# A two-block model kernel: loads in order of use, S5 by blocks, borders k by k, the tail by halves

## The chip, the cores and the metric

The kernel runs on one core of a Trainium2 chip. The metric is the device time of one execution in microseconds (us); the median of three runs is compared. A core has five engines with queues of their own that run in order: TensorE (PE in the profile) for matmuls, VectorE (DVE), ScalarE (ACT), GpSimd (POOL) and SyncE (SP), which here only issues DMAs. ACT and POOL issue DMAs too; in the profile ACTq and SPq are those issues. PSUM, where matmuls accumulate, is used as eight banks of 512 fp32 columns.

## What is computed

One sequence of 512 tokens, width 1024, goes through two different blocks, all in fp32:

```python
def first_block(x, c, ...):
    mod = (silu(c) @ w_ada + b_ada).reshape(Bsz, 6, D)      # shift, scale, gate, twice
    h = modulate(rmsnorm(x, norm_mix), shift_m, scale_m)
    proj = h @ w_in
    y_pool = pool_mixer(proj[..., :s_z], ...)
    y_ssd = ssd_mixer(proj[..., s_z:s_xbc], proj[..., s_xbc:s_dt], proj[..., s_dt:], ...)
    x = x + gate_m * (concatenate([y_pool, y_ssd]) @ w_out)
    h = modulate(rmsnorm(x, norm_ffn), shift_f, scale_f)
    x = x + gate_f * peer(h, w_query, sub_keys1, sub_keys2, expert_down, expert_up)
    return rmsnorm(x, norm_final)

def second_block(x, meta_tokens, ...):
    h = concatenate([meta, x])                              # 16 + 512 tokens
    proj = rmsnorm(h, g_mix_pre) @ w_in                     # q, k, v, r, a_low, u, z_gla, z_ssm
    o = gla_chunked(q, k, v, log_sigmoid(a_low @ w_gate_up + b_gate) / 16)
    y_gla = (rmsnorm(o, gla_norm_g) * silu(r)) @ w_o_gla
    y_s = s5_ssm(u, ...)                                    # x_t = Lbar x_{t-1} + Bbar u_t ; y = Re(C x) + D u
    glu = gelu(y_s) @ w_glu + b_glu
    y_ssm = glu[..., :D] * sigmoid(glu[..., D:])
    mixed = sigmoid(z_gla) * y_gla + sigmoid(z_ssm) * y_ssm
    h = h + rmsnorm(mixed @ w_out, g_mix_post)
    f = square(relu(rmsnorm(h, g_ffn_pre) @ w_ff1)) @ w_ff2
    return (h + rmsnorm(f, g_ffn_post))[:, N_META:]
```

PEER picks for each token 8 x 16 of 16384 experts by product keys; the S5 layer has 64 groups of 16 channels with 64 complex states each.

## The kernel before

Activations stand with channels on the 128 partitions and tokens along the columns, eight tiles of 128 channels, numbered k as input and m as output. An fp32 product is made of three matmuls in fp32r (`mm3`, lines 123 to 125): operands are split into hi and lo parts, and hi x hi, hi x lo and lo x hi are summed. A weight tile of 128 x 1024 is loaded by `load_w` on SP's queue into `raw` (three buffers) and split: hi on ACT (line 115), lo on DVE (line 116). One output tile of a projection (`linear`) takes 24 matmuls of 512 columns.

The stages, in order. The start: `ada` and `ada_pe` compute the modulation from 48 weight tiles (dot products on DVE, or on PE at line 220), the input is normalised, modulated and split k by k, and three projections have their weights loaded among the modulation's. Block 1: the input projection, pooling and SSD mixers, the output projection. PEER: the modulated h is transposed for 96 tokens through ACT copies (line 544) and PE transposes (545), query projections `wq`, top-16 searches, a dense pass over all experts' down weights (128 steps j), a dense pass over the up weights (128 j; `acc`, eight banks, is summed over j), and for the first 96 tokens gathered rows on POOL. At the end of the second pass gathered sums are folded into `acc` (line 1046) and added to the residual (1048). The dense pass's operand wg is split too (line 129).

Block 2: the meta tokens are normed (line 139's sums of squares of 16 columns), the residual is scaled and split into A (Ah, Al; line 1074), squares are summed on DVE (1081) and POOL, added over partitions with ones-matmuls (1085), and the factor `sc` that the projections' results are multiplied with follows. `proj(m, put)` makes a projection over 528 tokens in two pieces of 272 and 256 columns. Four heads of gated linear attention (GLA) come first; line 1151 is the gate's matmul.

S5 (lines 1263 to 1437). The eight projections of u are multiplied with `sc` and written to DRAM (`u_d`, POOL's queue); u is read back as `u4`, 16 channels of a group by 4 time offsets on the partitions, 32 pairs of groups (line 1320, eight reads on ACT's queue). Then for each of 16 steps of two pairs: `carry` loads `mat` (ACT's queue), transposes two tables (1343), makes the kernel kk (1350, 1351), spreads it with `selt` (1356) into the block table `tbd` (DVE, 1360 and 1364, the latter adds the skip), multiplies u into the carries (1370, 1371) and scans them on DVE; `answer` multiplies tables, states and u (1405 to 1407) and copies the result over u (1408). After each second step eight writes on SP's queue bring a block of y to DRAM (1424), and `glu_in` reads it back (1306), applies gelu (1308) and splits it. Between steps PE is kept busy with `lins`: gate projections (`gate_proj`, whose z goes through DRAM, lines 1281 and 1282) and attention output projections (`gla_out`).

Then the GLU (`wglu`), `wout2`, a norm, two halves of the FFN (`wff1`, `wff2`), a norm (products at line 1510, adds at 1511) and the output's write.

The order of the work is set by a scheduler (Tile): it takes instructions by priority in a simulated time. `soon()` and `high_priority` raise priorities, tile pools with a number of buffers set what waits for what. The row numbers of the instruction order, below, count an engine's instructions.

## Time and profile before

| | us |
|---|---|
| median of three runs | 2764.64 (2762.73 to 2776.26) |
| the profiled execution | 2769.02 |
| its span, first to last instruction | 2767.2 |
| PE busy | 2649.6 |
| DVE busy | 1899.2 |
| ACT busy | 1077.0 |
| POOL busy | 450.0 |

The span is that of one profiled execution; 1.8 us lie around it. The mean granted clock of PE is 0.98 of full speed. Idle time of an engine that is not the bottleneck costs nothing, so what matters is when PE does not work, and what it waits for then.

### The profile page before, as it was taken

The numbers are of one execution on the slowest core, as the hardware profiler recorded it, in microseconds if no ns is written. First come the engines' busy times: TensorE is split into PE (matmuls) and PEld (weight loads), VectorE is DVE, ScalarE is ACT, GpSimd is POOL, SyncE is SP. The second block draws the span as 40 slices with busy tenths as digits, with TensorE's granted clock in tenths as the row PEclk, the third lists the DMA queues.
The fourth block names the chain that finished last, engine by engine and source line by source line (L and its number), as shares of the span: only waits on it lengthen the run. The fifth ranks groups of instructions, "written<-read, shape, count | busy, mean of one in ns | idle before, by whom it ended". The sixth has DMA issues, their size and how long they took to land.

```text
span 2767.2 us, 36353 instructions
## 1 busy us (share of the span) xinstructions
PE 2649.6 (96%) x13812; PEld 2359.0 (85%) x13812; DVE 1899.2 (69%) x3456; ACT 1077.0 (39%) x1541; POOL 450.0 (16%) x361
## 2 busy tenths in 40 slices
PE   6999999999999999999999899899989989999997
PEld 5877789999999999999898899777878878688885
DVE  6767699998998873898698575744546754552543
ACT  5474434444445443333432232534422243432221
POOL 0010000443333030233314120100000100110100
PEclk9999999999999999999999999999999999999999
DMA  7224324888897577989977986111365644233231
GB/s 260 85 92 152 128 85 137 296 300 324 284 337 284 204 258 249 304 303 345 319 263 259 303 298 204 62 61 62 110 150 174 202 135 136 74 94 99 91 98 62
DMA packets 176064, 531.65 MB, mean 192 GB/s; under 512 B 18320, under 2 KB 55152, under 8 KB 173968
## 3 DMA queue, kind: packets, MB, share of 16 engines
q1 hardware_dynamic: 81152, 272.15, 29.5%
q0 software_dynamic: 36912, 152.39, 15.9%
q10 hardware_dynamic: 57824, 104.78, 11.5%
q8 instruction: 108, 1.77, 0.3%
q14 instruction: 68, 0.56, 0.1%
HBM read 448.74 MB, written 80.41 MB: 191 GB/s over the span
## 4 chain that ended last, share of the span: by engine, by line
PE 81%; DMA 6%; DVE 4%; issue 4%; ACT 3%; POOL 1%; ACTq 1%; SPq 0%; DVEq 0%; POOLq 0%
PE ps L123 24%; PE ps L124 24%; PE ps L125 24%; PE ps L701 4%; DMA gt<-g_d 2%; DMA row<-in_eu_dram,gid 2%; DVE lo L116 1%; PE ps L1240 1%; DMA mats_d<-bd 1%; ACT hi L115 1%; PE ps L1243 1%; PE ps L571 1%; DVE wg L1032 0%; PE ps L1356 0%; PE ps L139 0%
## 5 line engine op out<-in xcount | busy, mean ns | idle before, releaser
L115 ACT ACTIVATE hi<-raw 128x1024 fp32r<-128x1024 f32 (+1 forms) x458 | 481.8, 1053 | 1071.1 <-PE ps L124 772.9
L116 DVE TENSOR_TENSOR lo<-raw,hi 128x1024 fp32r<-128x1024 f32 (+1 forms) x458 | 582.9, 1273 | 332.2 <-ACT hi L115 327.7
L123 PE MATMUL ps<-h2h,hi 128*128 128x416 f32 (+1 forms) x1152 | 414.2, 360 | 0.7 <-ACT hi L115 0.7
L124 PE MATMUL ps<-h2l,hi 128*128 128x416 f32 (+1 forms) x1152 | 412.6, 358 | 0.0
L125 PE MATMUL ps<-h2h,lo 128*128 128x416 f32 (+1 forms) x1152 | 411.3, 358 | 0.0
L124 PE MATMUL ps<-wl,hi 128*128 128x416 f32 x1024 | 366.5, 358 | 24.0 <-DVE wl L129 24.0
L125 PE MATMUL ps<-wh,lo 128*128 128x416 f32 x1024 | 361.2, 357 | 1.8 <-DVE lo L116 1.8
L123 PE MATMUL ps<-wh,hi 128*128 128x416 f32 x1024 | 351.8, 355 | 5.7 <-ACT wh L128 4.6
L123 PE MATMUL ps<-Ah,hi 128*128 128x512 f32 (+2 forms) x944 | 342.5, 367 | 3.1 <-ACT Ah L128 3.1
L124 PE MATMUL ps<-Al,hi 128*128 128x512 f32 (+2 forms) x944 | 341.0, 361 | 0.0
L125 PE MATMUL ps<-Ah,lo 128*128 128x512 f32 (+2 forms) x944 | 340.1, 361 | 0.5 <-DVE lo L116 0.5
L712 POOL DMA_INDIRECT row<-in_eu_dram,gid x96 | 160.5, 1672 | 420.9 <-DVE tsum L735 360.9
L123 PEld LDWEIGHTS ps<-h2h,hi 128*128 128x128 f32 x1152 | 218.0, 189 | 7.5 <-ACT hi L115 1.2
L125 PEld LDWEIGHTS ps<-h2h,lo 128*128 128x128 f32 x1152 | 217.5, 189 | 6.8 <-DVE lo L116 0.3
L124 PEld LDWEIGHTS ps<-h2l,hi 128*128 128x128 f32 x1152 | 217.8, 189 | 6.1
L124 PEld LDWEIGHTS ps<-wl,hi 128*128 128x128 f32 x1024 | 195.8, 191 | 31.6 <-DVE wl L129 27.9
L123 PEld LDWEIGHTS ps<-Ah,hi 128*128 128x128 f32 x944 | 180.1, 191 | 38.6 <-issue 7.7
L125 PEld LDWEIGHTS ps<-Ah,lo 128*128 128x128 f32 x944 | 179.4, 190 | 33.6 <-issue 5.6
L124 PEld LDWEIGHTS ps<-Al,hi 128*128 128x128 f32 x944 | 179.9, 191 | 30.7 <-issue 4.0
L123 PEld LDWEIGHTS ps<-wh,hi 128*128 128x128 f32 x1024 | 196.3, 192 | 8.4 <-ACT wh L128 5.0
L125 PEld LDWEIGHTS ps<-wh,lo 128*128 128x128 f32 x1024 | 196.6, 192 | 3.8 <-DVE lo L116 2.5
L712 POOL DMA_INDIRECT row<-in_ed_r_dram,gid x96 | 146.2, 1523 | 214.2 <-DVE dots L720 185.3
(598 smaller groups left out, 4231.0 us busy)
## 6 DMA issues: line engine op xcount, KB each, us to landing
raw<-in_ed_dram SPq DMA_DIRECT2D x128, 512.0 KB
raw<-in_eu_dram SPq DMA_DIRECT2D x128, 512.0 KB
raw<-in_win_dram SPq DMA_DIRECT2D x74, 512.0 KB
raw<-in_wff_dram SPq DMA_DIRECT2D x64, 512.0 KB
g_d<-gst POOLq DMA_DIRECT2D x13, 2048.0 KB
aj<-act_d ACTq DMA_DIRECT2D x64, 416.0 KB
gt<-g_d ACTq DMA_DIRECT2D x45, 512.0 KB
wa<-in_wada_dram SPq DMA_DIRECT2D x44, 512.0 KB
```

What stands on the lines that cost most here:

```text
L115: top[0] = nc.scalar.activation(hi[:, :n], raw[:, :n], AF.Copy)
L116: low[0] = nc.vector.tensor_sub(lo[:, :n], raw[:, :n], hi[:, :n].bitcast(F32))
L123: nc.tensor.matmul(ps, wh, x[0], start=first, stop=False)
L124: nc.tensor.matmul(ps, wh, x[1], start=False, stop=False)
L125: nc.tensor.matmul(ps, wl, x[0], start=False, stop=last)
L571: nc.tensor.matmul(ps[:, t * P : t * P + P], q[:, t * P : t * P + P], skt[:, m], start=True, stop=True)
L701: nc.tensor.matmul(ps[:, i * P : i * P + P], o1[:, c, :, i], o2[a][:, c, :, i], start=a == 0, stop=a == 1)
L712: nc.gpsimd.indirect_dma_start(out=raw, out_offset=None, in_=src.rearrange("a b d -> (a b) d"), in_offset=bass.IndirectOffsetOnAxis(ap=gid ...
L1240: nc.tensor.matmul(po[hs], qx[:, c * 64 : c * 64 + 64], st, start=False, stop=True)
L1243: nc.tensor.matmul(ps, kt[hs, j], vt[hs, j], start=True, stop=True)
```

## The change

- Start: the first seven projections (`FIRST`) get their weights in k slices (`win_f`, 128 x 896, a second copy of the same weights), loaded between the modulation's tiles in order of use, and are accumulated k by k. Two modulation columns are made on PE instead of four. Later modulation loads wait for the last of these loads' issue.
- PEER: the 16 copies and transposes give way to 16 matmuls against the identity behind the seventh query projection (`tokens_of`), and six small copies on POOL's queue. The first three query projections run k by k (`linears`).
- The end of the second expert pass: the last two j are run d by d with the fold, and each d's residual follows.
- Block 2: projections 24 and 4 run k by k before the norm's sums, head 0's query projection before the norm's factor is used.
- S5: the eight u projections become part of the list of `lins`; each u block is written and read by itself, the reads (eight for each block) on SP's queue. Tables are made for four pairs at once, `mats_d` has another layout (wk, 4 x 288 columns, and em, 2 x 520), both read on SP's queue; the skip is added to kk; tbd is written by ACT. y's writes and reads move from SP's queue to POOL's. Ten `lins` are kept for after the last step.
- GLU and FFN: the split is made in place, the first two `wout2` and the first three `wff1` projections run k by k, the residual's adds are all on DVE.
- Tail: the last output's 48 matmuls run as two halves of 256 columns, each with its own norm, products, adds (all on DVE) and writes, on SP's and ACT's queues in turn.

```diff
-                if 2 <= k < 6:
-                    ada_pe(8 + k, a0)
+                if k in (2, 5):
+                    ada_here(8 + k, k)
...
+                wh, wl = load_w(I["win_f"][k], NF * P, ahead=False)
...
+                for i in range(NF):
+                    mm3(fp_[i], (wh, wl), (xh[:, k], xl[:, k]), k, k == 0, k == KD - 1, wk=i)
...
-                hd = tp.tile([P, q, n], F32, tag="t", name=nm("hd"))
-                nc.scalar.activation(hd, bc(t1[:, t0 : t0 + n].unsqueeze(1), [P, q, n]), AF.Identity, bias=shift)
-                nc.tensor.transpose(hps[g][k // 4][:, k % 4 * P : k % 4 * P + P], hd.rearrange("p a t -> p (a t)"), ident)
...
+        ahead = [psum("w") for _ in range(NQ)]
+        linears(ahead, [load_w(I["wq"][m]) for m in range(NQ)], (hh, hl))
...
+            if j < P - 2:
+                for d in range(KD):
+                    mm3(acc[d][:, TG:], w, (wh, wl), d, j == 0, False)
+            else:
+                held.append((w, (wh, wl)))
...
+    EARLY = (24, 4)
+    early = {m: (psum("w"), psum("w")) for m in EARLY}
+    we = [load_w(I["win2"][m], ahead=False) for m in EARLY]
+    for k in range(KD):
+        for m, w in zip(EARLY, we):
+            halves(early[m], w, k)
...
+        q0 = proj_x(0, "b")
...
-        usrc = u_d.rearrange("m (a g h) s c -> g s h (m a) c", a=4, g=2, h=16)
-        for g in range(2):
-            for s in range(LS):
-                p0 = 64 * g + 16 * s
-                nc.scalar.dma_start(u4[p0 : p0 + 16], usrc[g, s])
...
+            proj(25 + m, put)
+            with soon():
+                nc.gpsimd.dma_start(u_d[m], ub)
+                usrc = u_d[m].rearrange("(a g h) s c -> g s h a c", a=4, g=2, h=16)
+                for g in range(2):
+                    for s in range(LS):
+                        r0 = 64 * g + 16 * s
+                        nc.sync.dma_start(u4[r0 : r0 + 16, 4 * m : 4 * m + 4], usrc[g, s])
...
-        def carry(gi):
+        def tables(m):
...
-            nc.scalar.dma_start(mat[:, :n], mats_d[:, p0 : p0 + n])
+            wk = sp.tile([P, 4, WK], F32, tag="wk", name=nm("wk"))
+            nc.sync.dma_start(wk, mats_d[:, 4 * m : 4 * m + 4, :WK])
...
             for i in range(LS):
-                nc.tensor.matmul(ps[:, i * 16 * n : (i + 1) * 16 * n], selt[:, i], kk[:, : 16 * n], start=True, stop=True)
+                nc.tensor.matmul(ps[:, 64 * i : 64 * i + 64], selt[:, i], kk, start=True, stop=True)
...
-                nc.vector.tensor_copy(
+                nc.scalar.copy(
...
+        late = [lambda m=m: u_proj(m) for m in range(3, KD)]
+        rest, lins = lins, []
+        while rest:
+            if late:
+                lins.append(late.pop(0))
+            lins.append(rest.pop(0))
+        for m in range(3):
+            u_proj(m)
...
-                        nc.sync.dma_start(ydst[g, s], u4[r0 : r0 + 16, 4 * m : 4 * m + 4, 16 // LS :])
+                        nc.gpsimd.dma_start(ydst[g, s], u4[r0 : r0 + 16, 4 * m : 4 * m + 4, 16 // LS :])
...
-        nc.sync.dma_start(y, y_d[m])
+        nc.gpsimd.dma_start(y, y_d[m])
...
-        (nc.gpsimd if k % 8 in (1,3,5,7) else nc.vector).tensor_add(res[:, k], res[:, k], t)
+        nc.vector.tensor_add(res[:, k], res[:, k], t)
...
+        linears(ahead, wa_, hn, (k,))
+        sumsq(pss, res[:, k], k == 0, k == KD - 1)
...
+        H = T // 2
+        for c0 in (0, H):
+            c = slice(c0, c0 + H)
+            for kk in range(2):
+                for k in range(KD):
+                    mm3(ps[:, c], ws[kk], tuple(a[:, c] for a in f_of(kk * 8 + k)), k, kk == 0 and k == 0, kk == 1 and k == KD - 1)
...
+            for m in range(KD):
+                t = tp.tile([P, H], F32, tag="t", name=nm("fo"))
+                nc.vector.scalar_tensor_tensor(t, mx[:, m, c], col("g_ffn_post", m), rp[:, c], ALU.mult, ALU.mult)
+                nc.vector.tensor_add(t, t, res[:, m, c])
+                (nc.sync, nc.scalar)[m % 2].dma_start(out[m * P : m * P + P, c], t)
```

Three places of the instruction order on which the prediction rests. First PE where S5 begins. Before, the last matmuls of a gate projection (ps_18366) stand ahead of the first products of u, which is whole by then:

```order
L123 MATMUL ps_18366<-Ah_15598,hi_18368 128x512
L124 MATMUL ps_18366<-Al_15599,hi_18368 128x512
L125 MATMUL ps_18366<-Ah_15598,lo_18369 128x512
L1370 MATMUL ps_18088<-u_18043,sx_18065 128x132
L1371 MATMUL ps_18089<-u_18043,sx_18070 128x132
```

After the change, PE at the first S5 tables; ps_18647 and ps_18648 are the two pieces of the eighth and last u projection, wk is the table load:

```order
L126 MATMUL ps_18648<-Ah_15555,hi_18642 128x256
L127 MATMUL ps_18648<-Al_15556,hi_18642 128x256
L1413 MATMUL ps_17744<-ident,wk_17740 128x128 x4
L1413 MATMUL ps_17751<-ident,wk_17740 128x128 x4
L1421 MATMUL ps_17758<-wk_17740 128x16 x8
L128 MATMUL ps_18648<-Ah_15555,lo_18643 128x256
L126 MATMUL ps_18647<-Ah_15555,hi_18642 128x272
```

The tables' first matmuls now stand in the middle of the last u projection, and gate projections stand between the earlier u projections. Second, the queue of the u reads. Before, ACT, where they stand between small copies and the next weight split:

```order
L1345 COPY sx_18070<-ps_18067 128x256
L1353 COPY kk_18077<-ps_18072 128x32
L1320 DMA u_18043<-u_d 16x32x132 x8
L115 ACTIVATE hi_18469<-raw_18468 128x1024
L1281 ACT_TABLE_LOAD
```

After, SP; raw_18641 is the weight of the last u projection:

```order
L117 DMA raw_18641<-in_win_dram 128x1024
L1397 DMA u_17529<-u_d 16x4x132 x40
L1406 DMA wk_17740<-mats_d 128x4x288
L1408 DMA dk_17742<-in_dk_dram 128x64
L1439 DMA em_17776<-mats_d 128x2x520
L1406 DMA wk_17798<-mats_d 128x4x288
L1408 DMA dk_17800<-in_dk_dram 128x64
L1439 DMA em_17834<-mats_d 128x2x520
L1397 DMA u_17529<-u_d 16x4x132 x8
```

The reads of five blocks moved to SP as one run of forty, ahead of the table loads. Third, the end of S5. Before, SP carries y's writes and reads, the last three reads of a first group between two runs of writes:

```order
L1424 DMA y_d<-u_18043 16x4x128 x8
L1306 DMA y_19742<-y_d 128x512
L1306 DMA y_19748<-y_d 128x512
L1306 DMA y_19754<-y_d 128x512
L1424 DMA y_d<-u_18043 16x4x128 x8
L1306 DMA y_19760<-y_d 128x512
```

After, POOL carries them, with the gated attention's copies (yg_d) between:

```order
L1511 DMA y_d<-u_17529 16x4x128 x8
L1365 DMA y_19635<-y_d 128x512
L1351 DMA yg_d<-zg_19893 128x512
L1351 DMA yg_d<-zg_19928 128x512
L1511 DMA y_d<-u_17529 16x4x128 x8
L1365 DMA y_19641<-y_d 128x512
L1365 DMA y_19647<-y_d 128x512
```

One read of y stands ahead of the last eight writes instead of three; the other seven follow them.

## Rows read from the trace of the kernel before

**Rows 1.** The page, part 1: busy us (share) xinstructions of each engine.

```profile
PE 2649.6 (96%) x13812; PEld 2359.0 (85%) x13812; DVE 1899.2 (69%) x3456; ACT 1077.0 (39%) x1541; POOL 450.0 (16%) x361
```

**Rows 2.** Busy time by stretches: from:to, length, engines' busy us (instructions), PEclk, DMA share, GB/s.

```profile
2600.00:2640.00 40.00, 40.00 (x173) 32.08 (x172) 24.54 (x22) 12.02 (x15) 7.92 (x8) 1.00 0.30 92
...
0.00:75.00 75.00, 53.02 (x228) 41.97 (x229) 53.01 (x117) 41.67 (x56) 4.12 (x11) 0.98 0.67 247
...
1733.00:1770.00 37.00, 27.95 (x146) 24.37 (x146) 32.62 (x42) 20.80 (x42) 13.23 (x7) 0.82 0.14 43
2020.00:2045.00 25.00, 14.89 (x62) 12.31 (x62) 8.79 (x20) 5.18 (x7) 1.09 (x2) 0.80 1.04 143
2045.00:2220.00 175.00, 175.00 (x1031) 152.12 (x1030) 123.92 (x304) 46.94 (x88) 15.74 (x29) 1.00 0.51 171
...
2375.00:2392.00 17.00, 12.20 (x38) 7.62 (x37) 10.21 (x13) 7.52 (x13) 3.06 (x2) 0.90 0.20 62
2745.00:2767.20 22.20, 4.37 (x15) 2.31 (x13) 12.51 (x13) 1.95 (x3) 6.53 (x4) 0.71 0.25 95
...
2232.00:2242.00 10.00, 7.74 (x27) 6.66 (x28) 6.47 (x19) 5.59 (x8) 0.00 (x0) 0.50 0.30 89
```

**Rows 3.** PE's waits: line, what was waited for, us in total, times, longest.

```profile
PE ps L124 <- DVE wl L129: 24.0, 9, 6.0
...
PE ps L1370 <- DMA raw<-in_win_dram: 10.1, 1, 10.1
PE ps L139 <- ACT sq L138: 10.0, 5, 4.0
...
PE ps L545 <- ACT hd L544: 5.1, 5, 3.3
```

**Rows 4.** Busy time up to 74.6 us, of line 123 alone (columns PE, PEld).

```profile
0.00:74.60 74.60, 20.27 (x52) 10.86 (x52) 0.98 0.68 248
```

**Rows 5.** Timeline, PE, block 2's start: start, us, line, shapes [idle before <-releaser].

```profile
1753.74 1.12 PE L1085 MATMUL ps<-ms,ones 128*128 128x512 f32 x2 [1.67 <-DVE ms L1081]
1762.89 0.69 PE L1151 MATMUL ps<-al,wgu 16*128 16x272 f32 x2 [3.40 <-issue]
```

**Rows 6.** Timeline of ACT and of PE where S5 begins, and a stretch there.

```profile
2016.81 10.12 ACTq L1320 DMA_DIRECT2D u<-u_d  x8
2027.03 1.06 ACT L115 ACTIVATE hi<-raw 128x1024 fp32r<-128x1024 f32 x1 [12.20 <-DMA u<-u_d]
...
2039.44 0.78 PE L1370 MATMUL ps<-u,sx 128*128 128x132 f32 x2 [10.11 <-DMA raw<-in_win_dram]
...
2034.00:2044.00 10.00, 4.55 (x17) 4.20 (x18) 2.85 (x9) 0.74 (x2) 0.00 (x0) 0.50 0.86 191
```

**Rows 7.** Timeline of SP; then groups by line: busy us, mean ns | idle before.

```profile
2228.89 3.62 SPq L1424 DMA_DIRECT2D y_d<-u  x8
...
L1282 POOL DMA_DIRECT2D zs_d<-z x8 | 4.3, 543 | 53.5 <-ACT z L1281 32.4 <-ACT kk L1353 16.1 <-issue 5.0
...
L1356 PE MATMUL ps<-kk,selt 128*128 128x32 f32 x128 | 15.7, 266 | 0.3 <-ACT kk L1353 0.3
```

**Rows 8.** Timeline of PE and ACT at S5's end, and a piece of the chain.

```profile
2233.22 0.80 PE L1405 MATMUL ps<-u,tbd 128*128 128x128 f32 x2 [3.81 <-DVE tbd L1364]
2250.34 0.96 PE L123 MATMUL ps<-Ah,hi 128*128 128x512 f32 x3 [2.88 <-ACT Ah L128]
...
2236.74 1.28 ACT L1308 ACT_TABLE_LOAD   x1
...
2245.72 2.72 DMA y<-y_d
```

**Rows 9.** Timeline of PE at the norm before the FFN.

```profile
2385.31 1.93 PE L139 MATMUL ps<-sq,ones 128*128 128x512 f32 x2 [3.61 <-ACT sq L138]
```

**Rows 10.** Timeline of DVE from the last matmul to the end.

```profile
2747.42 0.69 DVE L1504 TENSOR_TENSOR mx<-mx,ps 128x512 f32<-128x512 f32 x1 [8.81 <-PE ps L125]
2751.37 9.41 DVE L1510 SCALAR_TENSOR_TENSOR fo<-mx,cols,rp 128x512 f32<-128x512 f32 x8 [3.26 <-ACT rp L165]
2760.70 2.49 DVE L1511 TENSOR_TENSOR fo<-fo,res 128x512 f32<-128x512 f32 x4
```

More of the change, by code (lines that the diff above doesn't have):

```diff
@@ L241, in tile_blocks, with ada_here @@
         rstd_of(rs, total(rs, res[:, KD - 1]), D)
-        xn = [tp.tile([P, T], F32, tag="t", name=nm("xn")) for _ in range(KD)]
+        NF = len(FIRST)
+        psa = psum()
+        fp_ = [psum("w") if i < 4 else psum() for i in range(NF)]
+        mods = {}
+        def ada_here(m, i):
+            wa = a0.tile([P, 1024], F32, tag="raw", name=nm("wa"))
+            nc.sync.dma_start(wa, I["wada_s"][m - 8])
+            for k in range(KD):
+                nc.tensor.matmul(psa[:, i : i + 1], wa[:, k * P : k * P + P], csc[:, k : k + 1], start=k == 0, stop=k == KD - 1)
+            nc.vector.tensor_add(mod[:, m : m + 1], psa[:, i : i + 1], col("b_ada", m))
+            ada_scale(m)
@@ L1381, in carry @@
             nc.vector.tensor_sub(vi, vi, a1)
-            for i in range(n):
+            for i in range(NG):
                 rb = bc(rho[:, p0 + i : p0 + i + 1], [P, NC5])
@@ L1451, in tile_blocks @@
         t = tp.tile([P, T], F32, tag="t", name=nm("ya"))
-        nc.vector.scalar_tensor_tensor(t, ps, col("b_glu", m), sb, ALU.add, ALU.mult)
-        nc.vector.tensor_add(mx[:, m], t, y)
-    mp = pair_tile("B", T)
-    for m in range(KD):
-        split(mx[:, m], mp[0][:, m], mp[1][:, m])
+        with soon():
+            nc.vector.scalar_tensor_tensor(t, ps, col("b_glu", m), sb, ALU.add, ALU.mult)
+            nc.vector.tensor_add(t, t, y)
+            split(t, mp[0][:, m], mp[1][:, m])
     rp = b2.tile([P, T], F32, name="rp")
     ln_exp()
+    ahead = [psum("w") for _ in range(2)]
+    linears(ahead, [load_w(I["wout2"][m]) for m in range(2)], mp)
     for m in range(KD):
-        ps = psum("w")
-        linear(ps, I["wout2"][m], mp)
+        if m < 2:
+            ps = ahead[m]
+        else:
+            ps = psum("w")
+            linear(ps, I["wout2"][m], mp)
         nc.scalar.copy(mx[:, m], ps)
@@ L1469, in tile_blocks @@
     pss = psum()
+    NA = 3
+    wa_ = [load_w(I["wff1"][m]) for m in range(NA)]
+    ahead = [psum("w") for _ in range(NA)]
     for k in range(KD):
@@ L1488, in tile_blocks @@
             for m in range(NH):
-                ps = psum("w")
-                linear(ps, I["wff1"][half * NH + m], hn)
+                if half == 0 and m < NA:
+                    ps = ahead[m]
+                else:
+                    ps = psum("w")
+                    linear(ps, I["wff1"][half * NH + m], hn)
                 t = tp.tile([P, T], F32, tag="t", name=nm("f"))
```

285 lines of the change are left out of this document (161 added, 124 removed).

## The prediction

> **What bounds the kernel now.** The page's first part shows TensorE (PE) busy for 2649.6 of 2767.2 us, 96% of the span [rows 1], so most of the time is matmul work that the change keeps: it is worth what it takes out of the waits of PE and out of PE's own small instructions. I read next the busy time by stretches [rows 2]. In 2600 to 2640 PE is full: 173 matmuls in 40 us, 0.231 us for one of 512 columns. The stretches where it is not full are the borders: the start (53.0 of 75 us busy), 1733 to 1770 where block 2 begins (28.0 of 37), 2020 to 2045 where S5 begins (14.9 of 25), 2375 to 2392 before the FFN (12.2 of 17), and the last 22.2 us (4.4). The third view, PE's waits [rows 3], says which are touched. The largest, 24.0 us for the split product of the dense expert pass, is not: I see the same order of that pass in both programs. The 10.1 us before the first S5 matmul, 10.0 us for squares before norms, and 5.1 us for the transposed copies in front of PEER are.
>
> Time is counted against the profiled execution, 2769.0 us (2767.2 span and 1.8 around it); it lies 4.4 us above the median of 2764.6, and I take the difference from the median. A measurement can tell about 0.5%, 13.8 us.
>
> **The change part by part.**
>
> Start. Seven projections in 168 matmuls now run k by k while their inputs appear. Before, 52 of line 123 had begun by 74.6 us [rows 4], so about four triples of the same seven projections were left, 12 x 0.231 = 2.8 us. Afterwards all seven can end about there, since inputs, loads (0.67 of the DMA engines' time in the first 75 us, [rows 2]) and the splits on VectorE (DVE) stay as they are and half of the modulation matmuls go. Against it: all eight PSUM banks are then full, and the next projection waits for a copy and a convolution step, 1 to 2 us. I take **+2 us** (a gain is positive here); bounds -4 (one more wait of the length of the block-2 start, below) and +6.
>
> PEER start. Sixteen transposes that waited 5.1 us [rows 3] go; sixteen matmuls of the same size and six small copies on POOL's queue come later, beside the query projections. But all eight modulated tiles on DVE now stand ahead of the first split, so PE waits there instead: **0**, -1 to +2.
>
> Block 2's start. In before PE idles 1.7 us for the sums, then 3.4 us before the gate matmul at 1762.9 [rows 5], and falls to a mean clock of 0.82 in the stretch [rows 2]. Now two projections run k by k from the first normalised k on, the squares come behind, and the query projection of head 0 (24 x 0.231 = 5.5 us) fills the time of the norm. ScalarE still does most squares and two weight splits ahead of the first input copy, so the first matmul comes hardly earlier. What is gained is the idle time plus part of the slow clock: **+6**, 2 to 10.
>
> S5 start, the largest term. Before, ScalarE's queue issued eight u read-backs of 264 KB from 2016.8 on, which took 10.1 us of it, held its next weight split for 12.2 us, and the first matmul that needs u began at 2039.4 after 10.1 us of waiting; the clock then stood at 0.50 to 2044, which costs 5 us more [rows 6]. 15.4 us is the stake. Afterwards u is read by blocks from SP. The order shows, though, that SP issues forty of the 64 small reads in one run, behind the weight load of the last u block and ahead of the first table's load. From the end of the fifth u block to the first table transposes PE has two u projections (48 x 264 columns, 5.7 us each), three gate projections (5.5 each) and a third of the last u block (2.0): 30 us. SP needs 2.5 us until the last weight buffer is free (one split on each of two engines), then 40 issues. Eight issues of the same size (16 rows by 4 pieces, a write) took 3.62 us [rows 7], 0.45 each, so 18.1 us; the transfers themselves, five eighths of the 22.6 us from 2016.8 to 2039.4, 14.1 us, fit under that. The table load lands 3 to 4 us later, at about 24.5 of 30 us: 5 us of cover are left. If that cover goes, each 0.1 us more for an issue costs 4 us. Behind the first table DVE makes kk, two groups of complex products and two weight splits in a row, and I allow 3 us of waiting: **+12**, 5 to 15.
>
> A rule speaks against this piece. The Trainium skill, "DMA: Bandwidth & Descriptors", section Bandwidth, calls transfers under 64 KB descriptor-dominated and gives each DMA about 2.0 us beyond its bytes. By it, taken one after another, 40 reads would last an estimated 83 us and the sum would turn into a loss; the eight 32 KB writes in 3.62 us [rows 7] say that such costs overlap, so I do not take it into the sum.
>
> S5's tables for four pairs. The selection matmuls halve in number (128 instructions with 15.7 us busy [rows 7] become 64 of twice the width). If an instruction costs the same, 7.8 us go; if by width, none; at these widths the mean hardly follows width, so **+6**, 0 to 8. Copies of the tables move from DVE to ScalarE, both with room (124 and 47 of 175 us in 2045 to 2220 [rows 2]): 0.
>
> S5's end. Before: 3.8 us for a table on DVE, 2.9 us for the gelu chain [rows 8], about 1.7 in smaller waits, and 5 us by the clock of 0.50 in 2232 to 2242 [rows 2]: 13.5 us. Afterwards the last answers lie among output projections of the gated attention, so the 3.8 goes. But the seven later reads of y stand on POOL's queue behind the last eight writes of y. At 0.54 us for an issue [rows 7] the second read starts 4.3 us after the last copy; with 0.54 of issue, 2.7 for the transfer (a read of the same size, [rows 8]), gelu 1.1 and its split 0.6 the second k arrives 9.3 us after the copy. The first k arrives after the table load of 1.28 us [rows 8], gelu and split, 3.1 us, and lasts 2.1. So PE idles 3.1 + 4.1 and then runs some microseconds at half clock, 3 to 5: 11 us stay. **+2.5**, -3 to +6.
>
> Norm before the FFN. PE waits 3.6 us for the first square there [rows 9] and more around it; three projections already interleaved before. Now the first product can go before the square, and half of the adds leave POOL: **+2**, 0 to 4.
>
> Tail. After the last matmul at 2747.4 come an add (0.69), square, two rsqrt steps, eight products in 9.41 us (1.18 each, with POOL adding beside) and adds up to 2763.2, and the last write lands at the end [rows 10]. Now the output's last 256 columns alone follow the last matmul; by the order eight half products and eight half adds of each half stand in blocks, and the second half's own add waits behind four adds of the first. At 0.35 to 0.4 us for a half I get 15 us after the last matmul instead of 19.8, which itself comes 0.9 us later for the extra ones-matmuls: **+4**, 1 to 7.
>
> Everything else keeps its work; the expert pass with its 24 us of waits for gathered data may come out 6 us either way. Sum: 2 + 0 + 6 + 12 + 6 + 2.5 + 2 + 4 = 34.5 us, 2769.0 to 2734.5 in the profile, and **2730** against the median.
>
> **The rivals.**
>
> A, the waits come back elsewhere: every edit at a border makes PE start earlier on pieces whose inputs come at the same pace from in-order ScalarE and DVE, so start, block 2, FFN and tail return 4 instead of 14, and S5's start 9. For it: DVE is busy 53.0 of the first 75 us [rows 2]. Against it: block 2's waits are for sums that no longer stand ahead of work. 2764.6 - 21.5 = 2743.
>
> B, S5's end gets worse: y's way over POOL is slower than reckoned by the low bound, and the first table is late by its bound: 2730 + 5.5 + 7 = 2743, near A. Both with other small losses reach 2752.
>
> C, slower: the small reads cost SP what the large ones cost ScalarE, 10.12 / 8 = 1.27 us [rows 6]. Then 40 take 50.6 us against 23.5 of room, a wait of 27 us, and the other 24, ahead of the next gate weight, 30.5 us against some 9.5 us of matmuls, 21 more; with twice 5 us of slow clock 58 us stand where 15.4 stood. The sum becomes 34.5 - 12 - 43 = -20: **2785**. It decides from 0.95 us for an issue on, where the losses eat all other gains. For it: runs of 528 bytes, read while weights load. Against it: 0.45 us for each write of the same shape. Its mechanism is the one that the rule quoted above describes, as far as issuing goes.
>
> D, the change does less than it says: the first S5 tables come after all u blocks and not among the first; that is in my cover already.
>
> **How the numbers follow.** Forecast 0.64; its own range is the terms' bounds taken as independent, 2717 to 2745. A 0.14, B 0.08, C 0.06 (D changes no number), and 0.08 for a better end than 2717 (no clock loss left at the borders, a lucky expert pass). The range for 8 in 10 goes from **2714 to 2753**. Faster by over 0.5% means below 2750.8: the forecast, the better end and somewhat under half of A and B's upper part, 0.81 in all; 0.13 within; 0.06 slower.
>
> **What would show it.** Right: no wait over 3 us before the first u matmul of S5 and a clock of 1.0 there; SP's forty reads issued within 20 us; a wait of 3 to 5 us in front of the second k of the GLU; under 16 us from the last matmul to the end; gate matmul of block 2 some 6 us earlier relative to the pass's end. Wrong: a new wait on a wk or weight load behind u reads, projections at the start that wait for PSUM, or the expert pass changing by over 6 us although its order did not.

## The result and the profile after

The changed kernel takes 2738.85 us (median of five runs, 2736.34 to 2745.07) against 2767.49 of the kernel before, run beside it: ratio 0.9886, interval 0.9866 to 0.9906. The forecast was 2730 in a range of 2714 to 2753. Direction and size hold; of the 9 us between, 3 are the kernel before, whose median came out at 2767.5 here against 2764.6, and 6 a smaller gain: 28.6 us instead of 34.5. The profiled execution has a span of 2734.7 us against 2767.2. First the page's part 1 and then PE's waits (line, what was waited for, us in total, times, longest; the largest, 14.7 us ahead of the start's first matmuls, is as before), which answer to [rows 1] and [rows 3]:

```profile
PE 2630.8 (96%) x13784; PEld 2349.5 (86%) x13784; DVE 1874.4 (69%) x3430; ACT 1070.8 (39%) x1510; POOL 491.1 (18%) x431
```

```profile
PE ps L128 <- DVE lo L119: 11.5, 4, 8.8
PE ps L127 <- DVE wl L132: 11.4, 4, 4.0
PE ps L126 <- ACT xh L131: 8.9, 2, 6.2
PE ps L126 <- ACT hi L118: 7.2, 5, 4.3
PE ps L126 <- ACT Ah L131: 7.0, 2, 3.5
...
PE ps L126 <- ACT Ah L1570: 3.7, 1, 3.7
PE ps L126 <- ACT Ah L1122: 3.0, 1, 3.0
```

The wait of 10.1 us for S5's first u matmul and the 10.0 for squares are gone or halved (sq has 5.6 left). In their place stand 4.3 for hi (S5's start), 2 x 3.5 for Ah (S5's end), 3.7 for Ah before the FFN and 3.0 for Ah at block 2's start. Two more lines are new. At the start 8.9 us for xh stand where 7.2 us for a weight's split stood. And 443 us into the second expert pass PE waits 8.8 us for a weight's split on DVE (lo), which stands behind DVE's additions of gathered rows. All twelve profiles of the changed order have this wait, from 7.2 to 8.8 us; the kernel before waited 7.0 us there in three pieces.

The stretches (from:to, length, busy us of PE, PEld, DVE, ACT, POOL with instructions, PEclk, DMA share, GB/s) are to be held against [rows 2]:

```profile
1728.00:1765.00 37.00, 31.27 (x198) 27.84 (x197) 26.19 (x35) 20.81 (x38) 6.25 (x6) 0.91 0.21 66
2010.00:2035.00 25.00, 20.69 (x150) 19.35 (x149) 8.17 (x20) 4.08 (x7) 1.62 (x3) 0.90 0.86 252
...
2210.00:2220.00 10.00, 6.58 (x19) 4.57 (x18) 2.27 (x4) 5.80 (x7) 4.81 (x10) 0.55 0.60 185
...
2712.00:2734.70 22.70, 8.24 (x58) 7.07 (x57) 12.63 (x34) 2.61 (x6) 0.00 (x0) 0.74 0.28 93
```

Block 2's start went from 28.0 of 37 us busy at 0.82 to 31.3 at 0.91, S5's start from 14.9 of 25 at 0.80 to 20.7 at 0.90, though its slow clock now lasts beyond the stretch, to 2040. The end of S5 still has a stretch at 0.55.

Most of the gain is in one part, from block 2's gate matmul to the last matmul of `wff1`. Its row in the kernel before, then in the changed kernel (same columns):

```profile
1762.89:2659.92 897.03, 873.06 (x4463) 714.40 (x4464) 479.52 (x787) 301.29 (x453) 63.93 (x77) 0.98 0.37 113
```

```profile
1757.82:2628.35 870.53, 853.65 (x4377) 701.96 (x4376) 459.71 (x733) 305.94 (x440) 92.49 (x145) 0.98 0.38 116
```

These 26.5 us divide as follows. The counts differ by 86 to 88, and by line these are 64 selection matmuls and the 24 matmuls of head 0's query projection, which now stand ahead of the gate. That projection's 5.5 us is only moved; it is paid in the stretch before. The selection matmuls are busy for 8.8 us instead of 15.7, 6.9 less. Idle time fell from 24.0 to 16.9, 7.1 us. The remaining 7.0 us of busy time are not a better clock: the granted clock is 0.98 in both rows, and PE was busy at 0.50 for 19.4 us of the first and for 18.0 of the second, which explains 0.7. The rest lies in matmuls of the same number at full clock: those of 512 columns that read Ah start 231 ns after one another instead of 235; those that read the attention's output, a third as many, went the other way, from 230 to 235. No run shows why.

Three things lie outside that row. The second expert pass, whose source the change leaves alone up to its last two j, lasted 621.3 us instead of 627.3, and from 616.3 to 629.5 in the runs below: 6 of the 32.5 us between these two profiles may be chance. The start gave 5 us up to the 160th matmul that reads xh, which is the 240th of the 600 projection matmuls (95.0 against 99.7 us), but nothing by the last one (225.0 against 224.2). And the tail, from the last `wff1` matmul to the end, took 106.3 us instead of 107.3.

### The profile page after: what moved, and what is told of

It reads as the page before. It is cut to its first block, busy times and chain, and to the rows that moved or that the text cites. A ratio compares the mean times of both kernels' runs of the same rounds, so it can differ in the third digit from the quotient of the medians.

```text
span 2734.7 us, 36390 instructions
## 1 busy us (share of the span) xinstructions
PE 2630.8 (96%) x13784; PEld 2349.5 (86%) x13784; DVE 1874.4 (69%) x3430; ACT 1070.8 (39%) x1510; POOL 491.1 (18%) x431
## 4 chain that ended last, share of the span: by engine, by line
PE 84%; DMA 6%; DVE 5%; issue 2%; ACT 2%; POOL 1%; ACTq 0%; SPq 0%; DVEq 0%; POOLq 0%
PE ps L127 24%; PE ps L126 24%; PE ps L128 24%; PE ps L745 4%; DMA gt<-g_d 3%; DMA row<-in_eu_dram,gid 1%; DVE lo L119 1%; PE ps L1307 1%; PE ps L1310 1%; DVE wg L1077 1%; PE ps L615 1%; PE ps L148 0%; PE ps L1421 0%; ACT hi L118 0%; PE ps L487 0%
## 5 line engine op out<-in xcount | busy, mean ns | idle before, releaser
L118 ACT ACTIVATE hi<-raw 128x1024 fp32r<-128x1024 f32 (+2 forms) x459 | 481.3, 1051 | 1068.0 <-PE ps L127 796.9
L119 DVE TENSOR_TENSOR lo<-raw,hi 128x1024 fp32r<-128x1024 f32 (+2 forms) x459 | 579.4, 1264 | 347.6 <-ACT hi L118 319.1
L128 PE MATMUL ps<-h2h,lo 128*128 128x416 f32 (+1 forms) x1152 | 411.2, 358 | 0.0
L128 PE MATMUL ps<-wh,lo 128*128 128x416 f32 x1024 | 358.4, 357 | 10.9 <-DVE lo L119 10.9
L756 POOL DMA_INDIRECT row<-in_eu_dram,gid x96 | 181.9, 1895 | 398.5 <-DVE tsum L779 329.6
```

What stands on the lines that cost most here:

```text
L118: top[0] = nc.scalar.activation(hi[:, :n], raw[:, :n], AF.Copy)
L119: low[0] = nc.vector.tensor_sub(lo[:, :n], raw[:, :n], hi[:, :n].bitcast(F32))
L128: nc.tensor.matmul(ps, wl, x[0], start=False, stop=last)
L756: nc.gpsimd.indirect_dma_start(out=raw, out_offset=None, in_=src.rearrange("a b d -> (a b) d"), in_offset=bass.IndirectOffsetOnAxis(ap=gid ...
```

## Experiments

All times of stretches are from the profiled executions. The measure for S5 and its borders is the time from the gate matmul to the last `wff1` matmul: 870.5 us in the changed kernel, 869.7 in its repeat.

**The changed kernel again.** No edit.

> The changed kernel itself, once more, as the measure for the others. It also tells how much the second expert pass varies from one execution to the next: the pass took 621.3 us in the profile of the changed kernel (first matmul 1107.2, last fold 1728.5) and 627.3 us before. Theory: its waits for gathered data are chance, so a repetition gives another value within some 6 us. Rival: the changed kernel's pass is shorter by its order, and the repetition gives 621 within 1 us.

Measured: 2739.37 us median (2730.89 to 2745.62), ratio 0.9894 (0.9872 to 0.9915). The first projection stage ended at 222.2 instead of 225.0 and the second pass took 619.7, the other stretches agree within about 1 us. So the start is known to some 3 us and, with the runs below, the second pass to some 13, and no term is read from one profile of them.

**S5's start: who holds the gate weight.** The theory was that the u reads which SP issues behind the first table hold back the next weight.

```
-                        nc.sync.dma_start(u4[r0 : r0 + 16, 4 * m : 4 * m + 4], usrc[g, s])
+                        (nc.gpsimd if m >= 5 else nc.sync).dma_start(u4[r0 : r0 + 16, 4 * m : 4 * m + 4], usrc[g, s])
```

> The changed kernel with the u reads of blocks 5 to 7 (24 of 64) issued from POOL's queue instead of SP's; nothing else is edited. Theory: in the changed kernel the wait of 4.3 us before the first gate projection among the S5 tables (PE for ACT's weight split, 2029.4 to 2034) and the half clock behind it (about 5 us) come from the weight load standing behind these reads in SP's queue: it was issued at 2028.8. Here it is issued by about 2017, the wait is under 1 us, the clock stays at 1.0, and S5 ends 6 to 10 us earlier. Rival: the chain of kk, complex products and splits on DVE is as late; then PE waits 3 to 4 us at the same place for DVE and the gain is under 3 us.

In the changed kernel, SP's queue, then ACT, then PE:

```profile
1990.54 21.45 SPq L1397 DMA_DIRECT2D u<-u_d  x40
2012.09 0.39 SPq L1406 DMA_DIRECT2D wk<-mats_d  x1
...
2015.61 7.18 SPq L1397 DMA_DIRECT2D u<-u_d  x8
...
2025.78 2.96 SPq L1397 DMA_DIRECT2D u<-u_d  x5
2028.84 2.73 SPq L117 DMA_DIRECT2D raw<-in_win_dram  x3
```

```profile
2032.86 1.06 ACT L118 ACTIVATE hi<-raw 128x1024 fp32r<-128x1024 f32 x1 [5.79 <-DMA raw<-in_win_dram]
...
2033.97 0.79 PE L126 MATMUL ps<-Ah,hi 128*128 128x512 f32 x1 [4.31 <-ACT hi L118]
```

The first table's load is issued at 2012.1, in time: its transposes wait for nothing. But sixteen further reads stand ahead of the weight load of 2028.84, and PE waits for the split of that weight. Eight of these reads take 7.18 us, although each is issued in 0.30 to 0.45: between them SP waits until the tables' loads, which it issued before, have landed (SP's waits from 2015.6 to 2022.9):

```profile
SPq L1397 <- DMA em<-mats_d: 1.7, 2, 1.0
SPq L1397 <- DMA wk<-mats_d: 1.7, 2, 1.3
SPq L1397 <- DMA dk<-in_dk_dram: 0.5, 1, 0.5
```

With the reads of blocks 5 to 7 on POOL the weight was issued at 2017.75, the wait fell from 4.3 to 0.2 and the clock stood at 1.00 from 2020 to 2040. The cause is shown. The time is 2734.62 (2732.49 to 2736.6), ratio 0.987 (0.985 to 0.9889), and from gate to last `wff1` 866.5. So 4 us were gained where the wait of 4.3 and the slow clock behind it (PE was busy for 6.4 us at 0.50, up to 2040, and about 3 of these are lost) had cost some 7. The rest came back at S5's end, PE's timeline and a stretch in this kernel:

```profile
2202.54 0.79 PE L1479 MATMUL ps<-s5xr,em 128*128 128x128 f32 x2 [2.90 <-DVE s5xr L1471]
2208.58 1.65 PE L126 MATMUL ps<-Ah,hi 128*128 128x512 f32 x3 [3.54 <-ACT Ah L131]
```

```profile
2200.00:2210.00 10.00, 3.92 (x13) 3.37 (x14) 3.51 (x8) 3.44 (x5) 5.32 (x11) 0.58 0.52 133
```

**S5's end: y reads behind y writes on POOL.**

```
-        nc.gpsimd.dma_start(y, y_d[m])
+        nc.sync.dma_start(y, y_d[m])
```

> The changed kernel with the eight reads of y issued from SP's queue again; the writes of y stay on POOL's. Theory: the wait of 3.6 us before the second k of the GLU's first projections (2211.9) is the reads' place behind the last eight writes on POOL's queue; it falls under 1 us, the wait before the first k (3.7 us, table load, gelu and split behind the last copy) stays, and the time from the last answer to the end falls by 3 to 6 us. Rival: the reads then stand behind GLU weight loads on SP and the wait only moves to the third or fifth k: gain under 1 us.

In the changed kernel, POOL, ACT and PE around the last answer:

```profile
2206.02 0.37 ACT L1481 COPY u<-ps 128x256 f32<-128x256 f32 x1 [0.29 <-PE ps L1480]
2206.41 1.28 ACT L1367 ACT_TABLE_LOAD   x1
2206.68 2.06 POOL L1511 DMA_DIRECT2D y_d<-u  x4 [0.25 <-ACT u L1481]
2207.70 1.10 ACT L1367 ACTIVATE g<-y 128x512 f32<-128x512 f32 x1
...
2209.01 2.03 POOL L1511 DMA_DIRECT2D y_d<-u  x4 [0.27 <-issue]
...
2209.52 0.96 PE L126 MATMUL ps<-Ah,hi 128*128 128x512 f32 x3 [3.54 <-ACT Ah L131]
2211.03 2.17 POOL L1365 DMA_DIRECT2D y<-y_d  x4
2214.10 1.10 ACT L1367 ACTIVATE g<-y 128x512 f32<-128x512 f32 x1 [4.63 <-DMA y<-y_d]
...
2215.91 0.80 PE L126 MATMUL ps<-Ah,hi 128*128 128x512 f32 x1 [3.42 <-ACT Ah L131]
```

The second y read starts when the eight writes are out, its gelu 8.1 us after the last copy. With y read through SP both waits are gone and the clock stays at 1.00 (last row below, against 0.55). 2728.57 us (2722.79 to 2732.51), ratio 0.9842 (0.9818 to 0.9866); from last answer to last `wff1` 411.2 instead of 422.6, 11 us where 3 to 6 were expected. The first wait, which I had put down to the gelu's table load, went as well: ACT now has that load ahead of the last copies, while PE still has projections (2205.40 here):

```profile
2205.40 1.28 ACT L1367 ACT_TABLE_LOAD   x1 [1.04 <-DMA y<-y_d]
...
2209.32 0.41 ACT L1481 COPY u<-ps 128x256 f32<-128x256 f32 x1
```

```profile
2210.00:2220.00 10.00, 10.00 (x50) 8.45 (x49) 4.50 (x6) 7.87 (x11) 4.64 (x9) 1.00 0.76 256
```

**Both queue edits together**, the two lines above in one kernel.

> The changed kernel with two of the earlier edits together: the u reads of blocks 5 to 7 issued from POOL, and the y reads issued from SP. Theory: the two waits on Ah at the end of S5 (7.0 us) and the wait on hi at its start (4.3 us) are separate losses with separate causes, so both go; between the first u matmul and the last answer the time stays at 178 to 181 us (what POOL's reads saved came back as a 2.9 us wait on DVE just before the last answer, since DVE is full there), and from the last answer to the last Ah it is 411 as with the y reads alone. Median 2726 to 2731, that is 8 to 13 us under the changed kernel. Rival: POOL's queue was what both edits relieved, y reads and u reads are in each other's way on it, and the second edit makes the first worthless: median 2728 to 2733 and a wait on hi of 4 to 6 us back at the start. Second rival: the DVE wait before the last answer grows since SP's y reads come earlier and add to the load at the end: over 4 us there, median above 2733.

2725.22 us (2724.02 to 2732.19), ratio 0.9836 (0.9819 to 0.9852); gate to last `wff1` 859.3 against 859.6 with the y reads alone. The wait for hi is gone, but a wait of 3.6 for Ah is back, now ahead of the last answer, and the clock of 2200 to 2210 is 0.78. Taking the wait at the start away gained 0.4 us in the profiles, less than two runs of one order differ by (1.7, below). Neither theory had it so: the waits have separate causes, but the second absorbs what the first releases.

**All u blocks first.** Is it the order, blocks of u among the projections, that makes S5's start cheaper?

```
-        late = [lambda m=m: u_proj(m) for m in range(3, KD)]
+        late = [lambda m=m: u_proj(m) for m in range(KD, KD)]
...
-        for m in range(3):
+        for m in range(KD):
             u_proj(m)
```

> The changed kernel with all eight u blocks projected ahead of the first table (in the changed kernel three, the other five among the other projections); tables for four pairs stay. All 64 u reads then stand on SP ahead of the first table's load. Theory: blocks among the projections are what takes the load of the first table out from behind the u reads; with all first, the table's load is issued only after the eighth block has been written and read (about 3 us for the write and 4.3 for its 8 reads after the projection's last matmul), so PE waits 6 to 12 us for the first tables or has to be fed by the weight loaded behind the 64 reads, and the clock falls to half for some microseconds after it: first u matmul to be reached 8 to 15 us later than the five more projections alone explain, time 2745 to 2753. Rival: the order of the u blocks is worth nothing, the gain of S5 comes from the tables for four pairs: no wait over 3 us there, time within 3 us of 2739.

SP and PE in this kernel, and two stretches at its S5's end:

```profile
1994.98 27.35 SPq L1397 DMA_DIRECT2D u<-u_d  x55
2022.43 0.36 SPq L117 DMA_DIRECT2D raw<-in_win_dram  x1
2022.89 0.39 SPq L1406 DMA_DIRECT2D wk<-mats_d  x1
```

```profile
2027.14 0.80 PE L126 MATMUL ps<-Ah,hi 128*128 128x512 f32 x1 [8.65 <-ACT hi L118]
```

```profile
2205.00:2215.00 10.00, 9.65 (x42) 7.24 (x41) 4.45 (x6) 5.40 (x7) 1.28 (x3) 1.00 0.70 228
2215.00:2225.00 10.00, 8.61 (x38) 6.72 (x37) 3.23 (x5) 7.17 (x9) 2.45 (x5) 1.00 0.43 160
```

The theory's wait is there: 8.7 us behind 55 reads in a row. Its price is paid, since the clock of 2020 to 2030 is 0.53, but more comes back: 2734.13 us (2728.08 to 2739.63), ratio 0.9863 (0.9841 to 0.9885), and 866.0 from gate to last `wff1`, 4.5 us less than in the changed kernel. The waits for Ah at S5's end are 1.4 us instead of 7.0, and the clock stays at 1.00 there. Neither the theory nor the rival had that.

**All u blocks first, their last reads on POOL.** This takes that wait of 8.7 us away and should show whether it can be had.

> All eight u blocks ahead of the first table and the u reads of blocks 5 to 7 issued from POOL; the y reads stay on POOL. Theory: the wait at the start of S5 goes as with the y reads on SP, and the end of S5 keeps its small wait of 1.4 us on Ah, since with fewer projections between the tables the answers are done earlier: gate to last Ah 856 to 860, median 2723 to 2729. Rival: POOL, which now has u reads ahead of the y writes, is late at the end of S5, and Ah is waited for 5 us or more there: 862 to 868, median 2730 to 2736.

2735.08 us (2728.84 to 2746.16), ratio 0.9876 (0.9853 to 0.9898); 866.2 us from gate to last `wff1`. No wait at the start, clock 1.00 there, and not a microsecond gained: PE waits 2.9 us for s5xr and 5.5 for Ah at the end instead. The matmuls of line 126 (a third of the projections') between the first u matmul and the last answer tell why. First with all blocks first, then with the reads on POOL, then the changed kernel:

```profile
2037.60:2195.65 158.05, 56.74 (x139) 26.21 (x139) 1.00 0.59 183
```

```profile
2027.79:2204.74 176.95, 64.27 (x160) 30.13 (x160) 0.99 0.58 183
```

```profile
2024.89:2205.71 180.82, 66.12 (x163) 31.09 (x163) 0.97 0.61 190
```

The source order of the first two is one and the same; only the queue of 24 reads differs. The scheduler, which orders by its simulated time, put 21 more of these matmuls (63 with lines 127 and 128, 14.6 us at 0.231 each) between the answers and so left fewer for after the last answer, where the chain answer, copy, y's write and read, gelu and split needs cover. That the edit changes the order is shown; that the scheduler did it because it saw the reads come earlier was not tried.

**All three together:** all u blocks first, late u reads on POOL, y reads on SP.

> All eight u blocks ahead of the first table, the u reads of blocks 5 to 7 issued from POOL and the y reads from SP. With all blocks first, PE stood 8.7 us at the start of S5 for a weight whose load came out behind 39 u reads that took SP 18.66 us. Theory: that wait is SP's queue and nothing else; with 24 of the 64 reads on POOL the weight and the first table's load come out in time, so the wait of 8.7 us falls under 2 us, the clock stays at full speed there, and with the y reads off POOL the end of S5 has no wait over 2 us on Ah: from the gate matmul to the last Ah 853 to 857 us (866.0 with all blocks first, 859.3 with both queue edits and three blocks first), median 2719 to 2725. Rival: what the start of S5 saves comes back at its end as a wait for the answers or for the gelu, as it did with the three-blocks order (0.2 us there, but 3.6 us on Ah and a half clock later): 858 to 862 us, median 2725 to 2730.

2725.25 us (2718.31 to 2732.2), ratio 0.9835 (0.9814 to 0.9856); 857.7. The start is clean (clock 1.00), one wait of 3.6 for Ah remains before the last answers. The rival has it, at the lower edge of its 858 to 862 and 2725 to 2730: it equals the version with three blocks first. These two are the fastest that were run, 13 to 14 us below the changed kernel.

**Twelve projections kept for the end** instead of ten, on the version with both queue edits.

```
-    AFTER = 10
+    AFTER = 12
```

> Both queue edits with three u blocks first, and twelve instead of ten projections kept for after the last answer. Theory: what the start of S5 saved came back because PE reaches the last answers and the first gelu ahead of DVE and ACT; two more projections of 5.5 us behind the last answer cover the 3.6 us on Ah, and the clock stays at full speed: gate to last Ah 853 to 856 against 859.3, median 2720 to 2724. Rival: with two fewer projections between the answers, PE waits for DVE's chain inside S5 instead, 3 us or more on s5xr or tbd: 859 to 863, median 2725 to 2730.

2727.53 us (2720.56 to 2736.27), ratio 0.9849 (0.9826 to 0.9871); 857.6. The wait of 3.6 us for Ah is still there, and the number of projection matmuls between first u matmul and last answer is 496 in both. The constant orders the source; the scheduler's order did not follow: every engine runs the same instructions in the same order from start to end. So this says nothing on its question, and it stays open whether more cover at the end would take the last wait away. It is a second run of the version with both queue edits, and tells how far two such runs differ: 2.3 us in the median (2725.22 there) and 1.7 in the stretch (859.3).

**Block 2's start undone.**

```
-    EARLY = (24, 4)
-    early = {m: (psum("w"), psum("w")) for m in EARLY}
...
+    early = {}
+    m3 = psum()
...
-    for m, acc_ in zip((m1, m2), sums):
-        nc.tensor.matmul(m, ones, acc_, start=True, stop=True)
+    with soon():
+        for m, acc_ in zip((m1, m2), sums):
+            nc.tensor.matmul(m, ones, acc_, start=True, stop=True)
...
-        q0 = proj_x(0, "b")
```

> The changed kernel with the start of block 2 put back: no projections of two tiles ahead of the norm, the column sums first and at high priority, head 0's query projection not started early. Theory (my term of +6, 2 to 10): the chain from the last fold to the first GLA matmul has idle time of PE which the early projections fill, so it takes 5 to 8 us more than the changed kernel's 64.9, with waits on Ah or on ms back in that stretch and a half clock after them; time 2743 to 2748. Rival: those waits are filled anyway and the projections only change places, so that the stretch is within 2 us of 64.9 and the time within 3 us of the changed kernel's 2739.

The stretch that I had named, last fold to first GLA matmul, is 67.0 us against 64.9, which would speak for the rival. It is the wrong stretch: 341 matmuls lie in it against 373, and the others follow later. Up to S5's first table transposes the work is the same (1683 and 1685 matmuls recorded), and there it takes 296.7 us against 290.2, and 289.0 to 290.4 in the seven other kernels with three u blocks first and the new start of block 2: **6.5 us**. Its two waits on PE, and the stretch to be held against the 31.27 us at 0.91 above:

```profile
1748.97 1.98 PE L1147 MATMUL ps<-ms,ones 128*128 128x512 f32 x4 [2.48 <-DVE ms L1143]
1755.86 1.24 PE L1213 MATMUL ps<-al,wgu 16*128 16x272 f32 x2 [4.90 <-issue]
```

```profile
1728.30:1765.30 37.00, 28.05 (x146) 23.34 (x146) 31.77 (x38) 22.59 (x38) 11.99 (x7) 0.82 0.21 66
```

The time, 2742.89 us (2734.82 to 2752.67), lies 4 us above the changed kernel's, which by itself is inside the scatter.

**The start undone.**

```
-    with tc.tile_pool(name="ada0", bufs=16, reuse_waits="tile") as a0:
+    with tc.tile_pool(name="ada0", bufs=6, reuse_waits="tile") as a0:
...
-                wh, wl = load_w(I["win_f"][k], NF * P, ahead=False)
...
-                for i in range(NF):
-                    mm3(fp_[i], (wh, wl), (xh[:, k], xl[:, k]), k, k == 0, k == KD - 1, wk=i)
...
+                if k < 3:
+                    m = (24, 20, 21)[k]
+                    first[m] = load_w(I["win"][m], ahead=False)
```

> The changed kernel with the start put back: the first weights loaded block by block of columns after the adaLN pieces as before, six buffers for raw weights, xn for all blocks ahead. Theory: the start is worth the 2 us of my sum, since the fill of 25 to 95 us is 5 to 7 us earlier in the changed kernel at the 160th matmul but most of it is given back by 225 us: 160th matmul at 99 to 100, last xh matmul at 224 to 226, time 2739 to 2742. Rival: the early part is worth what it shows, 5 to 7 us, and the profile of the changed kernel happened to lose it by chance later: last xh matmul at 227 to 230, time 2744 to 2747.

The 160th matmul that reads xh (the 160th of the expectation, the 240th of all) at 100.3, end of the stage at 224.7, against 92.1 to 95.0 and 222.1 to 225.0 in the kernels with the new start. 2738.45 us (2734.03 to 2744.43), ratio 0.9885 (0.9867 to 0.9903): no difference that can be measured. The rival's 5 to 7 us are refuted, the 2 us of the theory are an upper end.

**The tail undone.**

```
-        H = T // 2
-        for c0 in (0, H):
...
+        rstd_of(rp, total(rp, mx[:, KD - 1]), D)
+        for m in range(KD):
...
+            (nc.gpsimd if m in (0,1,3,5) else nc.vector).tensor_add(t, t, res[:, m])
```

> The changed kernel with the tail as before: the last output whole, products and adds over 512 columns, half of the adds on POOL, eight writes on SP. Theory: the halves bring only about 2 us: the last output takes 10.9 us on PE again instead of 13.4, and the end comes 20 us after its last matmul instead of 15; so this kernel is 1 to 3 us slower than the changed one. Rival: what the profile of the changed kernel lost before its last matmul lies elsewhere, and the halves are worth the whole 4 to 5 us.

2744.35 us (2736.67 to 2746.16), ratio 0.9896 (0.9872 to 0.992). From last `wff1` matmul to the end 109.6 us against 106.3 in the changed kernel and its repeat: undoing the halves costs 3.3 us. But the kernel before, with the same tail, took 107.3. The other 2.3 us lie in the rest of the change, and no run shows where. DVE in the changed kernel:

```profile
2712.74 0.42 DVE L1618 TENSOR_TENSOR mx<-mx,ps 128x256 f32<-128x256 f32 x1 [4.47 <-PE ps L128]
2717.43 3.26 DVE L1624 SCALAR_TENSOR_TENSOR fo<-mx,cols,rp 128x256 f32<-128x256 f32 x8 [4.27 <-ACT rp L174]
...
2725.56 3.26 DVE L1624 SCALAR_TENSOR_TENSOR fo<-mx,cols,rp 128x256 f32<-128x256 f32 x8 [1.85 <-ACT rp L174]
2728.73 2.77 DVE L1625 TENSOR_TENSOR fo<-fo,res 128x256 f32<-128x256 f32 x8
```

## Why the prediction was right, and which terms were not

**S5's start (+12, measured about +5).** The failed step is "The table load lands 3 to 4 us later, at about 24.5 of 30 us: 5 us of cover are left". That load did land in time, although the forty reads took 21.45 us and not 18.1: they were issued some 0.47 us apart, near the 0.45 that was reckoned, and SP waited 2.4 us between them. But I followed only the first load behind the reads. The next two blocks' reads stand ahead of the next weight load, and eight of them took 7.18 us, more than half of it waits for the tables' loads. PE waited 4.3 us there, with a half clock behind it, where [rows 6] had 10.1. My own sign of a wrong prediction, a new wait on a weight load behind u reads, is what came. Rival C had the place right and the price wrong: an issue took 0.30 to 0.45 us, not 1.27, and what held SP besides were landings, which neither C nor the sum has.

The stake was too large as well. In [rows 6] PE is busy for 4.55 us at the clock of 0.50, and not 5 us of that are lost but about 2, as matmuls of 512 columns show, which in the kernel before start 0.43 us apart at 0.50 and 0.23 at 1.00:

```profile
2042.62 0.63 PE L124 MATMUL ps<-Al,hi 128*128 128x512 f32 x1
2043.05 0.63 PE L125 MATMUL ps<-Ah,lo 128*128 128x512 f32 x1
...
2044.26 0.39 PE L125 MATMUL ps<-Ah,lo 128*128 128x512 f32 x1
2044.49 0.39 PE L123 MATMUL ps<-Ah,hi 128*128 128x512 f32 x1
```

So some 12 us stood there before and some 7 stand there now. In the same way the 5 us by the clock at S5's end were about 3.6 (PE busy for 7.7 of 10 us at 0.50).

The rule that I left out of the sum (the Trainium skill, "DMA: Bandwidth & Descriptors", section Bandwidth; the 2.0 us themselves stand in its section "Anatomy of one DMA — SWDGE (gpsimd) path", which puts most of them down to completion latency) does not add up here: forty reads of 33 KB were issued in 21.45 us from SP's queue, and the last of them had landed 23.0 us after the first was issued, against the estimated 83 us that its fixed cost would give in a row.

**Behind it, a step that I did not have:** a wait removed at S5's start is hardly worth its length, since PE then reaches the last answers and the gelu before they are ready. With three blocks first it brought 4 us of some 7 (reads of y on POOL) or 0.4 (on SP); with all blocks first 8.7 us of waiting went and nothing was gained. That is the mechanism of rival A, shown at this border.

**Selection matmuls (+6, measured +6.9):** their median is 275 ns at twice the width, 276 before, and 8.8 of the 15.7 us are left.

**S5's end (+2.5, measured about 2).** Of 8.5 us of waits in this place (3.8, 2.9 and smaller ones) 7.0 remain, 3.5 + 3.4 us where 3.1 + 4.1 were reckoned, and the clock of 0.55 follows. The chain was right step by step. What I missed is that it could be had for one word: reads of y on SP give 11 us.

**Block 2's start (+6, measured +6.5)** by undoing it. **Start (+2, measured -1 to +2.6).** The last projection matmul began at 222.1 to 225.0 us in the kernels with the new start, at 224.2 before and 224.7 with the start undone. **PEER's start (0, measured -1):** the first query matmul is 5.6 us earlier, the last 2.4 later, and the first expert pass ends 1.3 later. **The norm before the FFN (+2, measured 0):** 3.7 for Ah and 1.2 for squares stand where 3.6 and 1.2 stood: the first product goes first, but its input comes from the same ACT. **The tail (+4, measured 3.3 by undoing it, 1.0 against the kernel before):** after the last matmul 15.1 us, as reckoned; the extra cost on PE is 2.5 us, not 0.9, since the last output tile takes 13.4 us instead of 10.9 with its ones-matmuls and a wait of 0.5 for the add of the first half.

The prediction also has "I see the same order of that pass in both programs". For DVE that does not hold: where PE now waits 8.8 us, the splits of 1548.65 stand behind the additions of 1545.18 and 1546.94; at that place the kernel before has splits (1535.11, 1536.75) ahead of the addition of 1548.37.

So in the median 28.6 us came where 34.5 were summed, and in part that is luck. The terms as measured give only about 21: 7 us less at S5's start, 3 less at the tail, 2 less at the norm, 2 less at the start and PEER together, 1 more by the selection matmuls. The rest is most likely the 6 to 7 us by which matmuls of the same number are shorter in the long row; the sum does not have them, and their cause stays open. Of the signs named ahead, the wait before the second k (3.4) and the tail (15.1) came, no wait stands before the first u matmul, the gate matmul is as far from the pass's end as before (29.3 and 29.4 us) with 5.5 us more work between, and the forty reads took 1.5 us more than allowed.

Rivals A and B are not out by their total: 28.6 lies midway between the sum's 34.5 and A's 21.5. By its terms A is nearer to what came than the sum: start, block 2, FFN and tail gave about 8 us where the sum has 14 and A 4, and S5's start gave 5 where the sum has 12 and A 9. That the waits came back elsewhere is shown at S5; block 2's 6.5 us did not come back. B is out by its terms, since y's way over POOL cost 3.5 + 3.4 for 3.1 + 4.1 and the first table was in time. C is out by both. D is out too, since five blocks' reads stand ahead of the first table and three behind it.

## What to carry to other kernels

When small transfers go to an in-order queue, follow every load that stands behind them to its user, not the first one only: here the table was in time and the next weight was not. Count the large loads of the same queue too: SP's small reads waited for their landing. Price a removed wait by the next thing that PE will wait for, and hold work back as its cover; otherwise a clean start only brings PE sooner to the same chain. A simulated-time scheduler may reorder other engines when one DMA changes queue, so compare instruction counts between two fixed points before comparing times.

## What the runs showed of the hardware

The same reads of 33 KB were issued on SP every 0.50 us (27.35 for 55), 0.54 (21.45 for 40) or 0.90 (7.18 for 8), the last where loads of 520 to 576 KB had been issued just before. Each issue of the eight took 0.30 to 0.45 us; 3.9 us were waits for those loads and one of 32 KB to land. From 1990 to 2040 of the changed kernel SP never had more than eight of its transfers under way; whether the program or the queue sets that is not shown. On POOL y's writes stayed near 0.51 each (2.06 for 4).

PE's granted clock fell towards the lower level (1.2 GHz) after the two waits of 3.5 us around few matmuls (0.55 from 2210 to 2220), but stayed at 1.00 at S5's end in the kernel with all u blocks first, where in two stretches of 10 us PE idled 0.35 and 1.39 us. Behind that kernel's wait of 8.7 us at S5's start it was 0.53 from 2020 to 2030. At 0.50 matmuls of 512 columns started 0.43 us apart, at 1.00 0.23. The 7.0 us of waits for Ah were worth 11 with the clock behind them.
